# Second layer's first gates computed inside the attention projection's stage, and stage results stored through GpSimd's queue

## The chip, the core and the metric

The kernel runs on one core of a Trainium2 chip. A core has five engines, each with an instruction stream of its own, executed in order: TensorE (PE) multiplies matrices, VectorE (DVE) and ScalarE (ACT) work elementwise, GpSimd (POOL) does so more slowly, and SyncE (SP) issues most of the transfers between the chip's memory and the core's. GpSimd can issue transfers too, on a queue of its own. An instruction waits on semaphores for what it needs, and all behind it on its engine wait with it. The metric is the device time of one execution in microseconds, the median of several runs.

## The reference

One inference step of a two-layer trunk for two groups of requests: a prompt of 1024 positions, and 8 samples of 16 positions each, with width 1024 and everything in float32. Layer 0 mixes over time with an RWKV-7 recurrence. Layer 1 attends over a band: queries from its own projection, keys and values shared, computed once from the residual stream. Each layer ends in a gated feed-forward net. Cut to what the change touches:

```
def swiglu(h, w_gate, w_up, w_down):
    return (jax.nn.silu(h @ w_gate) * (h @ w_up)) @ w_down
...
for l in range(DEPTH):
    ...
    else:
        if l == N_A:
            k_new, v_new = shared_kv(x, c, ...)
        q = rms_norm((h @ p['wb_q'][j]).reshape(bsz, t, H_B, HEAD_B), p['q_norm'][j])
        o = band_attention(q, k_all, v_all, ...)
        out = o.reshape(bsz, t, d) @ p['wb_o'][j]
    x = x + gt_m[:, None, :] * out
    h = modulate(rms_norm(x, p['norm_ffn'][l]), sh_f, sc_f)
    x = x + gt_f[:, None, :] * swiglu(h, p['w_gate'][l], p['w_up'][l], p['w_down'][l])
```

## The kernel before

Activations lie feature-major: 128 features on the partitions, positions along the free dimension. The 1152 positions (1024 and 128 samples) are worked in two column halves, c=0 with 512 and c=1 with 640. A float32 product is made of three matmuls on rounded operands (`mm3`): `split` has ScalarE round a tile to `hi` (L330) and VectorE subtract it to get `lo` (L331).

The feed-forward net of a layer (`ffn`) runs over 22 groups f of hidden features. For each, `gate_up` makes seven products in place of eight by one step of Strassen's scheme. Their weights come from `strassen_weights(l, f)`: four loads of 256 KB (L1393), four additions (L1398 to L1401) and seven splits. Their other operands, B[c], come from `strassen_in`, once per half: eight loads of the normed residual X (L1351), the norm (`normed`: L411, and L419 to L421 for the samples), the combinations (L1357) and 28 splits. For the layer's f=0 the halves are computed apart, c=0 while c=1's operands are still being made; later groups do both at once. `gate_up` adds the products up (L1427), applies Silu and multiplies (L1441, L1443); its two results go to memory, s0 to the scratch tensor `bd`, s1 of f=0 to `b12` (`down_open`: `first`, `even` and `odd`, which make the second Strassen operands of each pair of groups). `down_sums` meanwhile prepares the weights of the down projection.

The stages in question follow one another: `kv` makes keys and values (to about 2400 us), `attention` runs the heads in pairs with the query projection and the first column half's output projection threaded between (to 2930), `attproj` does the second half's output projection in eight feature tiles n (to 2992), and then `ffn(1, ...)` begins. In `attproj`, `strassen_in` for c=0 advances by one step a tile (`next(sub, None)`), each tile's result is the residual plus the gated product (`residual`: L1228, L1232, L1233), is stored to `x3` (L2230), and its squares are added up for the next norm (`sq_add`, L369). After the last tile `sq_done` sums the squares over the partitions with a matmul against ones and takes the reciprocal root (`rsqrt2`, L391 and L392).

Results are stored from SP's queue: keys, values and queries (`head_tail`, `head_steps`, `out_v`, to the tensors out_kT, out_v and qT), attention outputs og (`heads_out`), the residual x3 (`proj_part`, `proj_rest`, `attproj`). Later loads read them back: the queries of the next pair of heads come as `h<-qT`, the attention outputs as `h<-og`.

The order of each engine's instructions is set at build time by a scheduler that simulates a timeline; the order in which the program is written gives the priority. On the chip each engine then takes its stream strictly in order. Tiles come from pools; a tile that takes the place of an older one waits for that one's last reader or writer.

## Time and profile before

| | us |
|---|---|
| median of 3 runs | 3776.3 |
| lowest and highest of them | 3771.32, 3779.6 |
| the profiled execution's own time | 3766.23 |
| its span, first to last instruction | 3764.4 |
| TensorE busy in the span | 3441.4 (91%) |
| VectorE, ScalarE, GpSimd busy | 2248.7, 1660.0, 787.5 |

The profile is of one execution. All durations below are of it, so a sum made from them stands against 3766.23, which is 10 us below the median of the runs. A line of a timeline gives the start, the duration, the engine, the line of the code (L12 is line 12), the operation, what is written and read, and in brackets the idle time before it with what ended it. SPq and POOLq mark the issue of transfers on SP's and GpSimd's queues. "Landing" is the time from the issue of a transfer to its completion.

### The profile page before, as it was taken

What the parts mean: (1) busy time and instruction counts of PE and PEld (TensorE: products, weight loads), DVE (VectorE), ACT (ScalarE), POOL (GpSimd) and SP (SyncE); (2) the same over time, 40 slices, a digit from 0 to 9 for tenths busy, and PEclk for the clock granted to TensorE, in tenths of its full rate; (3) what the DMA queues carried; (4) which work ended last, traced back from release to release, by engine and by line L of the source; (5) the groups of instructions that cost most, each with busy time, mean ns of one, the idle gap of its engine ahead of it and who ended that gap; (6) DMA issues with size and microseconds to landing.
All of it is one profiled execution on the core that took longest, in us unless ns stands there. A gap on an engine that the chain in (4) does not pass through costs nothing.

```text
span 3764.4 us, 74445 instructions
## 1 busy us (share of the span) xinstructions
PE 3441.4 (91%) x28982; PEld 3083.1 (82%) x28982; DVE 2248.7 (60%) x4366; ACT 1660.0 (44%) x3176; POOL 787.5 (21%) x775
## 2 busy tenths in 40 slices
PE   5888999999889799999999889789889899999999
PEld 4677778777667699999888869677667789999999
DVE  4667676765446765555446742666675675665655
ACT  5545556554223533333334542555564443333442
POOL 0000000000011066676100000000000146766200
PEclk9888899889699899999999999899999899999999
DMA  5776776677666444444889422445465434444764
GB/s 212 231 223 162 202 222 191 191 205 208 174 199 203 141 129 141 140 138 153 272 295 329 145 72 80 136 140 161 149 206 170 156 109 141 142 149 143 235 211 158
DMA packets 545938, 664.65 MB, mean 177 GB/s; under 512 B 137232, under 2 KB 405520, under 8 KB 541104
## 3 DMA queue, kind: packets, MB, share of 16 engines
q1 hardware_dynamic: 468736, 556.44, 46.5%
q0 software_dynamic: 23760, 85.08, 7.4%
q10 hardware_dynamic: 53088, 18.36, 2.1%
q8 instruction: 228, 3.74, 0.4%
q14 instruction: 126, 1.03, 0.1%
HBM read 483.18 MB, written 176.53 MB: 175 GB/s over the span
## 4 chain that ended last, share of the span: by engine, by line
PE 67%; DMA 13%; DVE 9%; issue 5%; ACT 4%; SPq 1%; POOL 1%; ACTq 0%; DVEq 0%; POOLq 0%
PE S L145 30%; PE PT L145 15%; PE acc L145 12%; PE st L145 3%; PE O L145 2%; PE G L145 1%; PE PT L2107 1%; PE aux L145 1%; DVE h L331 1%; PE Y L145 1%; DMA TT<-Z 1%; DMA raw<-in_wada 1%; DVE wlo L331 1%; DMA raw<-in_rw_o 1%; DMA aw<-in_wadb 1%
## 5 line engine op out<-in xcount | busy, mean ns | idle before, releaser
L145 PE MATMUL S<-h,w 128*128 128x256 f32 (+1 forms) x7374 | 1032.5, 299 | 24.8 <-ACT h L330 7.2
L145 PEld LDWEIGHTS S<-h,w 128*128 128x128 f32 x7374 | 1002.2, 191 | 43.2 <-issue 15.3
L330 ACT ACTIVATE w<-rq 128x512 fp32r<-128x512 f32 (+1 forms) x500 | 304.0, 614 | 645.8 <-PE S L145 259.6
L145 PE MATMUL acc<-mx,whi 128*128 128x384 f32 x1728 | 510.8, 373 | 31.6 <-ACT mx L330 12.3
L145 PE MATMUL PT<-h,w 128*128 128x256 f32 (+1 forms) x3714 | 527.4, 298 | 9.5 <-DVE h L331 3.5
L331 DVE TENSOR_TENSOR w<-rq,w 128x512 fp32r<-128x512 f32 (+1 forms) x500 | 384.7, 774 | 251.0 <-ACT w L330 212.6
L145 PEld LDWEIGHTS PT<-h,w 128*128 128x128 f32 x3714 | 505.3, 190 | 16.2 <-issue 6.5
L145 PEld LDWEIGHTS acc<-mx,whi 128*128 128x128 f32 x1728 | 339.7, 205 | 61.7 <-ACT mx L330 15.4
L145 PE MATMUL acc<-mx,wlo 128*128 128x384 f32 x864 | 318.0, 368 | 8.2 <-DVE wlo L331 8.2
L1427 POOL TENSOR_TENSOR t<-t,t 128x576 f32<-128x576 f32 (+1 forms) x132 | 221.9, 1683 | 263.0 <-ACT t L1434 153.3
L331 DVE TENSOR_TENSOR h<-h,h 128x1024 fp32r<-128x1024 f32 (+6 forms) x152 | 169.3, 1127 | 133.5 <-ACT h L330 120.6
L330 ACT ACTIVATE h<-h 128x1024 fp32r<-128x1024 f32 (+6 forms) x152 | 142.5, 950 | 158.8 <-DMA h<-bd 120.4
L145 PEld LDWEIGHTS acc<-mx,wlo 128*128 128x128 f32 x864 | 177.0, 205 | 19.7 <-DVE wlo L331 12.3
L331 DVE TENSOR_TENSOR wlo<-raw,whi 128x1024 fp32r<-128x1024 f32 x114 | 139.1, 1222 | 82.3 <-ACT whi L330 81.5
L330 ACT ACTIVATE whi<-raw 128x1024 fp32r<-128x1024 f32 x114 | 119.7, 1053 | 129.9 <-PE acc L145 73.0
L145 PE MATMUL S<-h,wh 128*128 128x320 f32 (+1 forms) x744 | 146.7, 351 | 19.5 <-ACT xo L1794 10.0
L145 PEld LDWEIGHTS S<-h,wh 128*128 128x128 f32 x744 | 123.6, 196 | 39.3 <-ACT xo L1794 15.8
L1427 DVE TENSOR_TENSOR t<-S,t 128x576 f32<-128x576 f32 (+1 forms) x117 | 86.7, 741 | 113.7 <-PE S L145 113.7
L145 PE MATMUL acc<-h,wh 128*128 128x256 f32 (+1 forms) x864 | 133.8, 303 | 3.5 <-DVE ht L391 1.3
L145 PEld LDWEIGHTS acc<-h,wh 128*128 128x128 f32 x864 | 118.0, 194 | 11.5 <-DVE ht L391 3.4
L1357 POOL TENSOR_TENSOR h<-h,h 128x256 f32<-128x256 f32 x12 | 10.7, 918 | 540.3 <-PE PT L145 540.3
L2108 ACT ACTIVATE pts<-PT 128x640 f32<-128x640 f32 (+4 forms) x128 | 72.6, 567 | 88.0 <-PE PT L2107 73.7
(480 smaller groups left out, 5536.4 us busy)
## 6 DMA issues: line engine op xcount, KB each, us to landing
bd<-t SPq DMA_DIRECT2D x154, 160.0 KB, 1.9
rq<-in_wg SPq DMA_DIRECT2D x88, 256.0 KB, 3.0
rq<-in_wu SPq DMA_DIRECT2D x88, 256.0 KB, 2.6
ws<-in_wd SPq DMA_DIRECT2D x64, 352.0 KB, 3.5
ws<-ws SPq DMA_DIRECT2D x64, 352.0 KB, 3.1
bd<-t SPq DMA_DIRECT2D x152, 128.0 KB, 1.8
rq<-ws SPq DMA_DIRECT2D x72, 256.0 KB, 3.2
h<-bd SPq DMA_DIRECT2D x28, 640.0 KB, 6.8
```

What stands on the lines that cost most here:

```text
L145: return nc.tensor.matmul(out, lhsT, rhs, start=start, stop=stop)
L330: self.nc.scalar.activation(hi, x, AF.Copy)
L331: self.nc.vector.tensor_tensor(lo, x, hi, ALU.subtract)
L1357: gp.tensor_tensor(out[j], x[j], y[j], op)
L1427: return eng.tensor_tensor(out, x, y, ALU.add)
L2107: nc.tensor.transpose(pt[:, j * 128:(j + 1) * 128], P[:, j * 128:(j + 1) * 128], self.C("ident"))
L2108: nc.scalar.activation(pts[:, 0:nk * 128], pt[:, 0:nk * 128], AF.Copy)
```

## The change

Two things are done.

First, f=0 of the second layer's gates, for c=0 only, is computed at the end of `attproj`. `early_weights` loads and splits its weights when the seventh feature tile (n=6) is written, into tiles that the attention no longer needs; c=0's operands are finished at the same point. After the reciprocal root, `gate_up` runs for c=0 with temporaries that lie in attention's buffers, its Silu behind the root's last ScalarE instruction. Its two stores go on GpSimd's queue. `ffn` for this layer then begins with f=2 (c=0, then c=1 after its operands), loads f=0's weights again for the missing c=1, and goes on with f=1, 3, 4 and so on to 21: 20 full groups in place of 21, over which the preparation of the down weights is spread. The first two pairs (f=0 with 1, f=2 with 3) reload the held half from memory; `b12` has two tensors.

Second, the stores named above (`head_tail`, `head_steps`, `out_v`, `proj_part`, `proj_rest`, `heads_out`, `attproj`) are issued by GpSimd in place of SP.

```diff
--- before.py
+++ after.py
@@ -387,7 +387,7 @@
         nc.scalar.activation(r, r, AF.Exp, scale=-0.5)
-        nc.scalar.activation(u, r, AF.Square, scale=float(n) ** -0.5)
+        self.rsq = nc.scalar.activation(u, r, AF.Square, scale=float(n) ** -0.5)
@@ -1303,6 +1303,7 @@
         self.halfraw = lambda: self.wq.tile([128, 512], F32, tag="rq", name=self.nm("rq"), bufs=5)
+        self.wtile = lambda: self.wq.tile([128, 512], F32R, tag="w", name=self.nm("w"), bufs=self.hw[2])
@@ -1383,7 +1384,7 @@
         def put(t):
-            hi, lo = (self.wq.tile([128, 512], F32R, tag="w", name=self.nm("w"), bufs=self.hw[2]) for _ in range(2))
+            hi, lo = (self.wtile() for _ in range(2))
@@ -1405,7 +1406,7 @@
 
-    def gate_up(self, put, B, W, cs):
+    def gate_up(self, put, B, W, cs, behind=None):
@@ -1429,7 +1430,8 @@
         add(dve, s0, product(1), t1)
-        nc.scalar.activation(s0, s0, AF.Silu)
+        with self.tc.issue_after(behind) if behind else ExitStack():
+            nc.scalar.activation(s0, s0, AF.Silu)
@@ -1446,14 +1448,18 @@
         nc = self.nc
-        spill = self.down_open(l)
-        self.gate_up(spill(0), B, iter(W), (0,))
+        spill = self.spill1 if l else self.down_open(l)
+        first = 2 if l else 0
+        self.gate_up(spill(first), B, iter(W), (0,))
...
             pass
-        self.gate_up(spill(0), B, iter(W), (1,))
-        for f in range(1, 22):
-            self.gate_up(spill(f), B, self.strassen_weights(l, f, nc.vector if f == 1 else None), (0, 1))
-            for g in range(32 * (f - 1) // 21, 32 * f // 21):
+        self.gate_up(spill(first), B, iter(W), (1,))
+        if l:
+            self.gate_up(spill(0), B, self.strassen_weights(l, 0, nc.vector), (1,))
+        for n, f in enumerate([1, *range(3, 22)] if l else range(1, 22)):
+            self.gate_up(spill(f), B, self.strassen_weights(l, f, nc.vector if l + n == 0 else None), (0, 1))
+            m = 20 if l else 21
+            for g in range(32 * n // m, 32 * (n + 1) // m):
@@ -1466,17 +1472,20 @@
         self.Ws = [self.dp.tile([128, 4, 1408], F32, name=f"ws{l}_{m}") for m in range(4)]
-        b12 = self.dp.tile([128, 576], F32, name=f"b12_{l}")
+        b12 = {p: self.dp.tile([128, 576], F32, name=f"b12_{l}_{p}") for p in range(l + 1)}
...
 
-        def first(s0, s1, cs):
-            c, = cs
-            nc.sync.dma_start(self.Bd[c][0][0][:, 0], s0)
-            nc.sync.dma_start(b12[:, part[c]], s1)
+        def first(p):
+            def f(s0, s1, cs):
+                c, = cs
+                q = nc.gpsimd if l and p + c == 0 else nc.sync
+                q.dma_start(self.Bd[c][0][0][:, p], s0)
+                q.dma_start(b12[p][:, part[c]], s1)
+            return f
@@ -1486,11 +1495,11 @@
             def f(s0, s1, cs):
-                if p == 0:
+                if p in b12:
...
                     for c in range(2):
-                        nc.sync.dma_start(held[0][:, part[c]], self.Bd[c][0][0][:, 0])
-                    nc.sync.dma_start(held[1], b12)
+                        nc.sync.dma_start(held[0][:, part[c]], self.Bd[c][0][0][:, p])
+                    nc.sync.dma_start(held[1], b12[p])
@@ -1504,7 +1513,7 @@
             return f
-        return lambda f: first if f == 0 else (odd if f % 2 else even)(f // 2)
+        return lambda f: (odd if f % 2 else first if f // 2 in b12 else even)(f // 2)
@@ -1775,12 +1784,11 @@
             with ExitStack() as c2:
-                A, st = self.attproj(B, x2, x3, self.attention(c2))
+                A, r = self.attproj(B, x2, x3, self.attention(c2))
...
                 self.wide_open2(c2, "1")
-                W = list(self.strassen_weights(1, 0, nc.vector))
-                r = self.sq_done(st)
+                W = list(self.strassen_weights(1, 2, nc.vector))
@@ -1824,7 +1832,7 @@
         yield from self.head_norm_steps(pz, m, g, x, self.one())
-        self.nc.sync.dma_start(dst, x)
+        self.nc.gpsimd.dma_start(dst, x)
@@ -1836,7 +1844,7 @@
         self.head_norm(pz, m, g, t, "acc")
-        self.nc.sync.dma_start(dst[:, n, 512 * c + o:512 * c + o + m], t)
+        self.nc.gpsimd.dma_start(dst[:, n, 512 * c + o:512 * c + o + m], t)
@@ -1891,7 +1899,7 @@
                     nc.scalar.activation(vt, pz, AF.Copy)
-                    nc.sync.dma_start(self.o["v"][4 * c + w, :, n * 256:(n + 1) * 256], vt)
+                    nc.gpsimd.dma_start(self.o["v"][4 * c + w, :, n * 256:(n + 1) * 256], vt)
@@ -1982,7 +1990,7 @@
                 self.residual(256, n, 64, t, x, pz)
-                self.nc.sync.dma_start(self.x3[:, n, o:o + 256], t)
+                self.nc.gpsimd.dma_start(self.x3[:, n, o:o + 256], t)
@@ -2006,7 +2014,7 @@
             self.residual(512, n, 64, x, x, pz)
-            nc.sync.dma_start(self.x3[:, n, 0:512], x)
+            nc.gpsimd.dma_start(self.x3[:, n, 0:512], x)
@@ -2127,7 +2135,7 @@
             nc.vector.tensor_copy(o[:, 0:w], O)
-            nc.sync.dma_start(self.og[n, :, t0:t0 + w], o[:, 0:w])
+            nc.gpsimd.dma_start(self.og[n, :, t0:t0 + w], o[:, 0:w])
@@ -2227,15 +2235,36 @@
             self.residual(512, n, 64, o, x, d)
-            nc.sync.dma_start(x3[:, n, self.cols(1)], o)
+            nc.gpsimd.dma_start(x3[:, n, self.cols(1)], o)
...
             next(sub, None)
-        for _ in sub:
-            pass
-        return A, st
+            if n == 6:
+                for _ in sub:
+                    pass
+                W0 = self.early_weights()
+        r = self.sq_done(st, self.rs[:, 0:640])
+        ends = iter([self.at.tile([128, 320], F32, tag=t, name=self.nm("t"), bufs=b) for t, b in [("ht", 5)] * 5 + [("xin", 2)]])
+        self.halfraw = lambda: next(ends)
+        self.spill1 = self.down_open(1)
+        self.gate_up(self.spill1(0), B, iter(W0), (0,), self.rsq.ins)
+        return A, r
+
+    def early_weights(self):
+
+        wide = [self.slot(1)[:, :1024] for _ in range(3)]
+        raws = iter([t[:, o:o + 512] for t in wide for o in (0, 512)])
+        pieces = [self.att("kc", [128, 4, 512], 1, F32R).rearrange("p a b -> p (a b)"),
+                  self.att("vc", [128, 4, 4, 128], 1, F32R).rearrange("p a b c -> p (a b c)"),
+                  self.slot(1, F32R)[:, :1024], self.slot(1, F32R)[:, :1024],
+                  *(self.att("bt", [128, 641], 3, F32R)[:, :512] for _ in range(2))]
+        tiles = iter([t[:, o:o + 512] for t in pieces for o in range(0, t.shape[-1], 512)])
+        self.halfraw, self.wtile, old = lambda: next(raws), lambda: next(tiles), self.halfraw
+        W = list(self.strassen_weights(1, 0, self.nc.vector))
+        self.halfraw = old
+        return W
```

Lines after the change are numbered by its own code: L1394 to L1402 stand for L1393 to L1401, L1428 for L1427, L1443 and L1445 for L1441 and L1443, L1352 for L1351, L1358 for L1357, and from attention on they are 8 higher.

The order of the instructions at three places. VectorE behind the residual of the projection's last tile, before the change; o is the tile's result, kk and rms the squares and the root, w and rq the weights' low parts and raw halves, x the loads X, h in the first row the sum of squares:

```order
L1233 TENSOR_TENSOR o_32737<-o_32737,x_32736 128x128
L369 TENSOR_TENSOR h_31922<-h_31922,kk_32743 128x640
L331 TENSOR_TENSOR w_32762<-rq_32753,w_32761 128x512
L331 TENSOR_TENSOR w_32766<-rq_32755,w_32765 128x512
L1398 TENSOR_TENSOR rq_32769<-rq_32757,rq_32759 128x512
L1399 TENSOR_TENSOR rq_32757<-rq_32753,rq_32757 128x512
L391 SCALAR_TENSOR_TENSOR kk_32798<-S_32794,kk_32798 128x640
L1400 TENSOR_TENSOR rq_32753<-rq_32769,rq_32753 128x512
L392 SCALAR_TENSOR_TENSOR rms_32797<-kk_32798,rms_32797 128x640
L1401 TENSOR_TENSOR rq_32755<-rq_32755,rq_32753 128x512
L419 TENSOR_TENSOR x_32804<-x_32804,rms_32797 128x128
```

The split of the next weights follows the sum of squares directly there. VectorE at the same place with the change; t are the early gate's temporaries, and the root lies in h_31922:

```order
L1233 TENSOR_TENSOR o_32768<-o_32768,x_32767 128x128
L369 TENSOR_TENSOR h_31922<-h_31922,kk_32774 128x640
L1428 TENSOR_TENSOR t_32787<-PT_32854,t_32786 128x256
L391 SCALAR_TENSOR_TENSOR kk_32780<-S_32777,kk_32780 128x640
L392 SCALAR_TENSOR_TENSOR h_31922<-kk_32780,h_31922 128x640
L1428 TENSOR_TENSOR t_32790<-PT_32897,t_32786 128x256
L1428 TENSOR_TENSOR t_32791<-S_32914,t_32790 128x256
L1443 TENSOR_TENSOR t_32788<-t_32788,t_32789 128x256
L1428 TENSOR_TENSOR t_32791<-S_32930,t_32791 128x256
L1445 TENSOR_TENSOR t_32787<-t_32787,t_32791 128x256
L331 TENSOR_TENSOR w_32963<-rq_32954,w_32962 128x512
L331 TENSOR_TENSOR w_32967<-rq_32956,w_32966 128x512
```

All additions of f=0's first half now stand ahead of the first weight split, which in both pieces is the first row with L331.

SP at the loads of X for c=1, before, with the semaphores that each row waits for (DMAHW are transfers of SP's queue, DMASW of GpSimd's; the others are engines):

```order
L1514 DMA ws_33723<-in_wd 128x4x176 [waits DMAHW6_49]
L1351 DMA x_32804<-x_110 128x640 [waits DMAHW7_49]
L1351 DMA x_32805<-x_110 128x640 [waits DMAHW0_49]
L1351 DMA x_32806<-x_110 128x640 [waits DMAHW1_49]
L1351 DMA x_32807<-x_110 128x640 [waits DMAHW2_49]
```

They wait for earlier transfers of SP's queue alone. SP at the same place with the change:

```order
L1394 DMA rq_32960<-in_wu 128x512
L1352 DMA x_32995<-x_110 128x640 [waits DMAHW4_49,PE_49]
L1352 DMA x_32996<-x_110 128x640 [waits DMAHW5_49,DMASW0_49,DVE_49]
L1352 DMA x_32997<-x_110 128x640 [waits DMAHW6_49,Activation_49]
L1352 DMA x_32998<-x_110 128x640 [waits DMAHW7_49,DMASW1_49,DVE_49]
```

The second and the fourth load now wait for transfers of GpSimd's queue and for VectorE: they use the buffers of the early gate's s1 and s0, whose stores are on that queue.

SP at one boundary between pairs of heads, before; bt, kc, vc, vn are biases and cached keys and values, og<-o, qT<-xin the stores of attention outputs and queries:

```order
L2040 DMA bt_29719<-in_rel 128x641
L2130 DMA og<-o_28887 128x128
L2130 DMA og<-o_28950 128x256
L1839 DMA qT<-xin_28953 128x320
L1927 DMA h_29028<-qT 64x1024
L1920 DMA h_29665<-out_kT 64x1024 x2
L2155 DMA kc_29412<-in_ck 128x2048
L2140 DMA qsm_29778<-qT 128x128
```

Three stores stand ahead of the load of the queries. SP at the same place with the change:

```order
L2165 DMA vn_29111<-out_v 16x4x128
L2048 DMA bt_29719<-in_rel 128x641
L1935 DMA h_29028<-qT 64x1024
L1928 DMA h_29665<-out_kT 64x1024 x2
L1935 DMA h_29670<-qT 64x1024
L2163 DMA kc_29412<-in_ck 128x2048
L2148 DMA qsm_29778<-qT 128x128
```

The three stores are gone from SP; the load of the queries, h<-qT, still stands ahead of the loads of the next pair, and that of the second half of the pair now also stands ahead of kc. GpSimd's stream, where the stores of that place now are:

```order
L1847 DMA qT<-xin_28784 128x320
L2138 DMA og<-o_28887 128x128
L1847 DMA qT<-xin_28953 128x320
L2138 DMA og<-o_28950 128x256
L1847 DMA qT<-xin_29188 128x256
```

They stand there in one row with no other work between them.

## The prediction

> **What bounds the kernel now.** The page comes first: its head, the busy times, and the chain that ended last.
>
> ```profile
> span 3764.4 us, 74445 instructions
> ...
> PE 3441.4 (91%) x28982; PEld 3083.1 (82%) x28982; DVE 2248.7 (60%) x4366; ACT 1660.0 (44%) x3176; POOL 787.5 (21%) x775
> ...
> PE 67%; DMA 13%; DVE 9%; issue 5%; ACT 4%; SPq 1%; POOL 1%; ACTq 0%; DVEq 0%; POOLq 0%
> ```
>
> TensorE is busy for 91% of the span and holds 67% of the chain, so an edit pays only where TensorE waits now. The table of stretches, cut at the stages that the change touches, shows where (microseconds, busy time and instructions of each engine, granted clock, DMA share, GB/s):
>
> ```profile
> 2500.00:2600.00 100.00, 91.08 (x795) 73.16 (x793) 64.48 (x192) 61.21 (x142) 0.00 (x0) 0.93 0.48 147
> ...
> 2985.00:3000.00 15.00, 11.68 (x66) 9.91 (x66) 5.52 (x10) 4.54 (x7) 0.00 (x0) 0.89 0.41 139
> 3000.00:3010.00 10.00, 3.92 (x23) 3.49 (x23) 9.48 (x21) 5.54 (x12) 0.00 (x0) 0.78 0.81 298
> 3010.00:3020.00 10.00, 7.43 (x51) 7.02 (x50) 10.00 (x28) 8.24 (x17) 1.11 (x1) 0.88 0.00 0
> 3020.00:3030.00 10.00, 5.92 (x37) 5.43 (x37) 10.00 (x26) 5.84 (x14) 2.61 (x2) 1.00 0.34 109
> 3030.00:3043.00 13.00, 10.99 (x49) 9.84 (x50) 12.61 (x30) 5.47 (x14) 2.11 (x2) 0.74 0.06 19
> ...
> 3100.00:3500.00 400.00, 400.00 (x3009) 400.00 (x3008) 235.88 (x271) 131.26 (x217) 273.87 (x230) 1.00 0.46 145
> ```
>
> Between the projection and the second layer's gates, from 3000 to 3043, VectorE is the full engine (9.48 of 10, then 10.00, 10.00 and 12.61 of 13) and TensorE the one that waits. In the gates' steady loop it is the reverse: 400.00 of 400 on TensorE. There 3009 matmuls take 400 us, 0.133 us each. One feature group f of the gates has 168 matmuls (7 products, 4 slices, 3 matmuls, two halves c), so a full f costs 22.3 us, and, divided by columns (256 to 320), c=0 9.9 us and c=1 12.4 us. TensorE's timeline around the transition:
>
> ```profile
> 2987.74 4.27 PE L145 MATMUL PT<-h,wh 128*128 128x320 f32 x28
> 2995.16 2.24 PE L145 MATMUL S<-h,cst 128*128 128x320 f32 x4 [3.15 <-DVE h L369]
> 2997.58 2.41 PE L145 MATMUL S<-h,w 128*128 128x256 f32 x12 [0.18 <-ACT w L330]
> ...
> 3042.75 6.66 PE L145 MATMUL S<-h,w 128*128 128x256 f32 x48
> ```
>
> Call the end of the projection's matmuls T = 2987.74 + 4.27 = 2992.0. From T, TensorE needs 2.24 us for the sum of squares and 22.3 us for f=0, and f=1 starts at 3042.75 = T+50.7. So 26 us are lost here, and this is what the early gates aim at. VectorE's timeline gives the cause:
>
> ```profile
> 3000.48 0.69 DVE L1398 TENSOR_TENSOR rq<-rq,rq 128x512 f32<-128x512 f32 x1 [1.00 <-DMA rq<-in_wu]
> ...
> 3041.33 0.48 DVE L331 TENSOR_TENSOR h<-x,h 128x320 fp32r<-128x320 f32 x1
> ```
>
> From 3000.48 (T+8.5) to the last split of c=1's operands at 3041.8 VectorE runs 41.3 us without a gap.
>
> **The change part by part.** *Projection.* Group f=0's weights are now loaded and split during the last feature tiles: 7 splits and 4 additions on VectorE, 7 copies on ScalarE, 4 loads of 256 KB on SP's queue. What VectorE does there now, by form, in 2950 to 2992:
>
> ```profile
> L331 DVE TENSOR_TENSOR h<-h,h 128x256 fp32r<-128x256 f32 x14 | 8.3, 642 | 0.4 <-ACT h L330 0.4
> L331 DVE TENSOR_TENSOR wh<-vf,wh 128x512 fp32r<-128x512 f32 x9 | 6.5, 726 | 8.9 <-ACT wh L330 8.9
> ```
>
> Added is 7 x 0.73 + 4 x 0.69 = 7.9 us to some 25 us of 42 (these rows and the smaller ones), so it fits beside TensorE, which is the busier one. A split that lands ahead of a tile's own can hold it up by one or two: I take +0.5 us on T; bounds 0 and +3 (four such hold-ups).
>
> *After T.* Counting VectorE's rows in the changed order: the tile's residual, the sum of squares, then everything that ends f=0's first half, and only then the first weight split of f=2. So TensorE first does the ones product (T+3.2 to T+5.4, as now) and six of c=0's seven products, 6 x 1.42 us, to T+13.9, or T+14.4 with the clock of 0.89 that the row of 2985 to 3000 shows for part of it. Two additions on GpSimd and two on VectorE follow, and VectorE turns to f=2 at T+16.3, where it started on f=0 at T+8.5 before. Its block until the last operand split is of the same kinds: two more weight splits, three fewer additions, and the two rows of the reciprocal root gone; 39.5 us in place of 41.3. To that comes a new wait. The loads of X, eight in a row,
>
> ```profile
> 2997.01 5.91 SPq L1351 DMA_DIRECT2D x<-x  x8
> ```
>
> need buffers that the early gate's temporaries held: the second waits for the store of the gate's s1 on GpSimd's queue, the fourth for that of s0, and the other six stand behind them on SP. The store is issued at T+15.8. What a store costs on each queue I read from these rows (2100 to 3050; size, median us from issue to landing):
>
> ```profile
> x<-x SPq DMA_DIRECT2D x16, 320.0 KB, 4.3
> ...
> x<-xin SPq DMA_DIRECT2D x16, 128.0 KB, 3.3
> ...
> qT<-xin SPq DMA_DIRECT2D x12, 160.0 KB, 1.8
> ...
> x<-h POOLq DMA_DIRECT2D x6, 128.0 KB, 2.7
> ```
>
> 2.7 us to land and 4.3 us for the load behind it: the second X is there at T+22.8, while VectorE has run out of other work at T+20.5. It idles 2.3 us. The block then ends at T+16.3+39.5+2.3 = T+58.1; f=2's last product ends 1 us later, as now (3041.8 against 3042.75), and f=0's second half needs 12.4 us: T+71.5 with two groups done. Before, two groups are done at T+50.7+22.3 = T+73.0. **The gates' part gains 1.5 us**, not the 9.9 us of the products moved: VectorE, which binds, begins 7.8 us later. Bounds: a gain of 4 (no wait for X), a loss of 3 (7.1 us for the store in place of 2.7, the longest landing below).
>
> *Steady loop.* f=0's weights are loaded and split a second time (1 MB, 5 us of VectorE), f=3 reloads its held pair, and the sums for the down weights spread over 20 rounds. TensorE covers all: VectorE is at 235.88 of 400 there and the DMA engines at 0.46. Zero. If cover failed, it would be in the 12.4 us of a lone c=1 half, where 7 splits and some 2 us of additions still fit:
>
> ```profile
> L331 DVE TENSOR_TENSOR w<-rq,w 128x512 fp32r<-128x512 f32 x126 | 106.6, 846 | 63.1 <-ACT w L330 44.0 <-PE S L145 12.7 <-PE PT L145 6.4
> ```
>
> *The stores.* In the kv projection and attention they leave SP for GpSimd, which is idle (0.00 in the row of 2500 to 2600). Each costs it 542 ns of issue:
>
> ```profile
> L1588 POOL DMA_DIRECT2D x<-h x32: 542/542/587, 1869.5 to 2134.4; - x32
> ...
> DMA to landing us min/median/max: 2.4/3.6/7.1
> ```
>
> It counts where a load reads what a store has just written. The chain of waits in attention has such places:
>
> ```profile
> 2405.47 1.76 DMA qT<-xo
> 2407.93 4.20 DMA h<-qT
> ...
> 2601.63 1.76 DMA qT<-xin
> 2603.45 3.49 DMA h<-qT
> ...
> 2779.07 1.80 DMA qT<-xin
> 2780.95 3.39 DMA h<-qT
> ...
> 2850.04 3.75 DMA h<-og
> ...
> 2911.07 3.21 DMA x<-xin
> 2914.30 4.23 DMA h<-x
> ```
>
> About seven in all (five pair boundaries with qT, one with og, one with x). The store lands in 1.76 to 1.80 us on SP; on GpSimd's queue, 2.7 by the nearest row, so +0.9 each and 6 us if each stood bare. SP is relieved in turn: it no longer stops for results, and loads that stand behind a store go out when their own buffer is free. But the loads of qT stay ahead of the bias, cache and value loads in its order, and they wait for the landing. About half of the places had slack or gain from a free SP: I take **+2 us**; bounds +12.6 (3.6 against 1.8, seven times) and -8 (below).
>
> [...]
>
> **Sum.** +0.5 - 1.5 + 0 + 2 = +1.0 us, on the profiled execution's own 3766.2: 3767.2. That execution was 10 us (0.27%) below the median of 3776.3, a spread of runs and not of the work, so the term goes on the median: **3777**.
>
> **The rivals.** *Free SP* (faster). If the stores were what held the loads up, the four long waits of TensorE that DMA ends at pair boundaries shrink. For: on SP, og's stores land anywhere from 1.7 to 9.6 us,
>
> ```profile
> DMA to landing us min/median/max: 1.7/2.6/9.6
> ```
>
> TensorE's idle times there, in the brackets:
>
> ```profile
> 2413.31 0.69 PE L145 MATMUL S<-h,h 128*128 128x128 f32 x2 [7.18 <-DVE h L331]
> ...
> 2535.31 1.43 PE L145 MATMUL acc<-ht,cst 128*128 128x320 f32 x2 [2.31 <-ACT ht L1797]
> ...
> 2666.94 0.33 PE L2107 MATMUL PT<-cst,P 128*128 128x128 f32 x1 [3.30 <-ACT pts L2108]
> ...
> 2724.14 1.33 PE L2107 MATMUL PT<-cst,P 128*128 128x128 f32 x5 [3.69 <-ACT pts L2108]
> ```
>
> Half of these 16.5 us is -8; with the gates at -1.5 and the projection at +0.5, -9: 3767. Against: qT's loads still wait in SP's order for the very stores that moved.
>
> *Late stores* (slower). The seven places pay the other row's median, 3.6 against 1.8, +12.6, and X comes 0.9 us later: -1.5 + 0.9 + 0.5 + 12.6 = +12.5, 3789. It decides as soon as a store on GpSimd's queue lands 1.4 us later than on SP at all seven places (+10 and more). For: the row of 2.4/3.6/7.1. Against: the six of 2.7 nearest in time, and 3.3 us for SP's own stores of x.
>
> *No gain from the gates.* If X waits longer (7.1 us for the store, loss of 3), the sum is +5.5, 3782: still no change that can be told.
>
> **How the numbers follow.** A measurement of this kernel can tell about 0.2%, 7.5 us, from no change. Free SP 0.22; late stores 0.27; the rest, forecast and lost gates, 0.51. Faster 0.23, same 0.50, slower 0.27. The range takes in both rivals with 3 us beyond each: 3764 to 3792.
>
> **What would show it.** Right: VectorE's first weight split of f=2 about 16 us after the projection's last matmul, a wait of it for X of 2 to 3 us, and two groups done 70 to 73 us after T; qT's stores landing in 2.5 to 3 us. Wrong: if the two groups are done before T+68, the block of VectorE was shorter than counted; if TensorE's idle time from 2400 to 2930 falls by 5 us or more, SP's waits were the bound; if it grows by 8, the landing was. The steady loop must stay at a full TensorE.

## The result, and the profile after

The change makes the kernel **slower by 0.51%**: 3795.69 us, the median of 8 runs (3784.47 to 3807.43), against 3776.8 us, the median of 8 runs of the kernel before. The ratio is 1.0051 with a 95% interval of 1.0033 to 1.0068, so 12 to 26 us. The forecast of 3777 is wrong, and 3795.69 lies above its range.

The page of the changed kernel, its head, TensorE's busy time and the chain that ended last (the execution's own time is 3805.07 us):

```profile
span 3803.3 us, 74561 instructions
...
PE 3455.2 (91%) x28982; PEld 3090.9 (81%) x28982; DVE 2263.4 (60%) x4383; ACT 1665.9 (44%) x3188; POOL 884.7 (23%) x937
...
PE 57%; issue 18%; DMA 10%; DVE 9%; ACT 3%; POOL 2%; SPq 1%; ACTq 0%; POOLq 0%; DVEq 0%
```

The same 28982 matmuls take 13.8 us more, and the span grows by 38.9. The two busy shares look alike; where the time went is read from rows at the same place of the program in both. TensorE's timeline, first before, then after: attention's first matmul of a query head, its last one of a pair, and (after alone; before's are in the prediction) the projection's last matmuls and the first ones behind two finished groups of gates.

```profile
2405.01 1.12 PE L145 MATMUL O<-h,cst 128*128 128x512 f32 x2 [1.31 <-ACT h L1797]
...
2881.90 1.08 PE L145 MATMUL PT<-vc,pts 128*32 128x128 f32 x32 [0.85 <-ACT pts L2108]
```

```profile
2421.30 1.12 PE L145 MATMUL O<-h,cst 128*128 128x512 f32 x2 [1.31 <-ACT h L1805]
...
2915.02 1.08 PE L145 MATMUL PT<-vc,pts 128*32 128x128 f32 x32 [0.85 <-ACT pts L2116]
...
3021.34 7.20 PE L145 MATMUL PT<-h,wh 128*128 128x320 f32 x48
...
3098.64 3.36 PE L145 MATMUL PT<-h,w 128*128 128x256 f32 x24
...
3136.74 4.99 PE L145 MATMUL S<-h,w 128*128 128x256 f32 x24 [1.95 <-DVE t L1428]
```

| stretch | before, us | after, us | difference |
|---|---|---|---|
| up to attention's first row | 2405.0 | 2421.3 | +16.3 |
| attention, first row to last | 476.9 | 493.7 | +16.8 |
| to the projection's last matmul, T (2992.0 and 3028.5) | 110.1 | 113.5 | +3.4 |
| T to two groups of gates done | 73.0 | 70.1 | -2.9 |
| from there to the end | 699.3 | 704.7 | +5.4 |

The first stretch is almost all unchanged code, and this execution is 9 us above its own median. A kernel below whose code is before's up to there (before with late pins) has 2417.9 us in it, so most of those 16 us are the spread of executions. Attention is where the change shows, though the spread of executions is in its 16.8 us too. Cut at TensorE's rows `PT<-vn,pts`, about 4.4 us of it lie in attention's first piece, ahead of every place that is looked at below, 3.6 in the second, 2.3 at the boundary where ScalarE stands longest, 4.4 at the last boundary and 3.6 in the two pieces that end the stage; the other pieces together give some 1.5 back. Take the last boundary first. Between two marks there (the rows `PT<-vn,pts` that begin at 2769.26 and 2792.43 before, 2794.25 and 2821.82 after), the table of stretches has, before and then after (us, busy time and instructions of PE, PEld, DVE, ACT, POOL, granted clock, DMA share, GB/s):

```profile
2769.20:2792.40 23.20, 18.18 (x189) 12.80 (x181) 14.95 (x52) 14.48 (x36) 0.00 (x0) 1.00 0.78 265
```

```profile
2794.20:2821.90 27.70, 22.21 (x191) 16.06 (x189) 14.88 (x50) 15.70 (x36) 2.17 (x4) 0.82 0.80 274
```

From row to row the same piece costs 4.4 us more, and TensorE's busy time in the two stretches differs by 4.0: TensorE stands once, and comes back at a lower clock. Both are 14.1 us behind the first mark when it begins to wait; the wait is 2.6 us longer after, and the rows behind it take 1.8 us more. The same columns in slices, after:

```profile
2806.00:2809.00 3.00, 2.38 (x21) 1.36 (x21) 1.71 (x7) 0.70 (x1) 0.00 (x0) 1.00 0.63 147
2809.00:2812.00 3.00, 0.52 (x3) 0.30 (x5) 1.13 (x1) 2.22 (x4) 0.00 (x0) 0.73 0.90 343
2812.00:2815.00 3.00, 3.00 (x22) 2.67 (x22) 1.20 (x5) 0.84 (x5) 0.00 (x0) 0.50 1.05 399
2815.00:2818.00 3.00, 3.00 (x14) 1.94 (x13) 1.64 (x6) 1.68 (x4) 0.54 (x1) 0.50 1.05 386
```

ScalarE's timeline of the piece says why TensorE stands, before and then after:

```profile
2780.90 0.70 ACT L2108 ACTIVATE pts<-PT 128x640 f32<-128x640 f32 x1 [0.64 <-PE O L145]
...
2783.15 0.70 ACT L2108 ACTIVATE pts<-PT 128x640 f32<-128x640 f32 x1 [1.54 <-PE PT L2107]
...
2784.36 1.06 ACT L330 ACTIVATE h<-h 64x1024 fp32r<-64x1024 f32 x1 [0.51 <-DMA h<-qT]
```

```profile
2806.08 0.70 ACT L2116 ACTIVATE pts<-PT 128x640 f32<-128x640 f32 x1 [1.86 <-PE O L145]
2809.78 1.06 ACT L330 ACTIVATE h<-h 64x1024 fp32r<-64x1024 f32 x1 [3.00 <-DMA h<-qT]
2810.74 0.68 ACT L2116 ACTIVATE pts<-PT 128x640 f32<-128x640 f32 x1
```

The row `ACT L330 h<-h 64x1024` of each is the point. It is `split`'s rounding of the next pair's queries, just loaded back from `qT`. Before, it stands behind both `pts` copies (the transposed softmax of the present pair); after, **one of them stands behind it**. The load has not landed and ScalarE takes its stream in order, so it stands 3.00 us, the ready `pts` with it, and TensorE, which needs that copy:

```profile
2811.48 0.48 PE L2115 MATMUL PT<-cst,P 128*128 128x128 f32 x1 [3.10 <-ACT pts L2116]
```

At the same row before TensorE had waited 0.49. At another boundary ScalarE stands longer (ScalarE, TensorE, and the issue of the store and of the load behind it, after; TensorE's wait there was 3.30 us before, a row that the prediction shows):

```profile
2685.99 1.06 ACT L330 ACTIVATE h<-h 64x1024 fp32r<-64x1024 f32 x1 [7.89 <-DMA h<-qT]
2686.95 0.68 ACT L2116 ACTIVATE pts<-PT 128x640 f32<-128x640 f32 x1
```

```profile
2687.69 1.33 PE L2115 MATMUL PT<-cst,P 128*128 128x128 f32 x5 [5.00 <-ACT pts L2116]
```

```profile
2680.13 0.54 POOL L1847 DMA_DIRECT2D qT<-xin  x1 [3.77 <-DVE xin L1811]
```

```profile
2682.40 0.46 SPq L1935 DMA_DIRECT2D h<-qT  x1
```

The load is issued 2.27 us behind the store, and ScalarE goes on 3.6 us after that. Nothing is unusual in the transfers: before, this store was issued at 2656.84 and its load at 2658.96, 2.12 us, and the store landed in 2.1 us on either queue. ScalarE was sent to wait sooner: it began to wait at 2678.10, 2.0 us ahead of the store's issue, where before it had come 4.5 us behind it (at 2661.34, for 1.29 us). Over the attention, ScalarE's wait for these loads (total us, times, longest), before and after:

```profile
ACT h L330 <- DMA h<-qT: 15.1, 8, 6.0
```

```profile
ACT h L330 <- DMA h<-qT: 24.1, 8, 7.9
```

And the landing itself, on GpSimd's queue (KB each, median us):

```profile
og<-o POOLq DMA_DIRECT2D x28, 128.0 KB, 2.2
...
qT<-xin POOLq DMA_DIRECT2D x12, 160.0 KB, 2.1
...
qT<-xin POOLq DMA_DIRECT2D x12, 128.0 KB, 2.2
```

Before, the same three were 2.3, 1.8 and 1.7 on SP.

### The profile page after: what moved, and what is told of

Read it like the earlier page. It is cut to its first block, busy times and chain, and to the rows that moved or that the text cites. A ratio compares the mean times of both kernels' runs of the same rounds, so it can differ in the third digit from the quotient of the medians.

```text
span 3803.3 us, 74561 instructions
## 1 busy us (share of the span) xinstructions
PE 3455.2 (91%) x28982; PEld 3090.9 (81%) x28982; DVE 2263.4 (60%) x4383; ACT 1665.9 (44%) x3188; POOL 884.7 (23%) x937
## 4 chain that ended last, share of the span: by engine, by line
PE 57%; issue 18%; DMA 10%; DVE 9%; ACT 3%; POOL 2%; SPq 1%; ACTq 0%; POOLq 0%; DVEq 0%
PE S L145 27%; PE PT L145 13%; PE acc L145 9%; PE st L145 3%; PE G L145 1%; DVE h L331 1%; PE aux L145 1%; DMA TT<-Z 1%; PE O L145 1%; DVE w L331 1%; PE Y L145 1%; DVE wlo L331 1%; DMA raw<-in_rw_o 1%; DMA Z<-T 1%; DMA h<-bd 1%
## 5 line engine op out<-in xcount | busy, mean ns | idle before, releaser
L145 PE MATMUL S<-h,w 128*128 128x320 f32 (+1 forms) x7314 | 1027.8, 299 | 31.4 <-ACT h L330 7.9
L330 ACT ACTIVATE w<-rq 128x512 fp32r<-128x512 f32 (+1 forms) x500 | 304.0, 615 | 623.4 <-PE S L145 263.9
L331 DVE TENSOR_TENSOR w<-rq,w 128x512 fp32r<-128x512 f32 (+1 forms) x500 | 393.7, 793 | 249.6 <-ACT w L330 219.6
L1428 POOL TENSOR_TENSOR t<-t,t 128x576 f32<-128x576 f32 (+2 forms) x135 | 225.6, 1672 | 267.7 <-ACT t L1436 169.6
L331 DVE TENSOR_TENSOR h<-h,h 128x1024 fp32r<-128x1024 f32 (+7 forms) x154 | 170.7, 1123 | 143.2 <-ACT h L330 136.5
L330 ACT ACTIVATE h<-h 128x1024 fp32r<-128x1024 f32 (+6 forms) x154 | 143.7, 947 | 175.6 <-DMA h<-bd 125.7
L331 DVE TENSOR_TENSOR wlo<-raw,whi 128x1024 fp32r<-128x1024 f32 x114 | 139.3, 1223 | 88.8 <-ACT whi L330 87.8
L330 ACT ACTIVATE whi<-raw 128x1024 fp32r<-128x1024 f32 x114 | 119.8, 1055 | 139.4 <-PE acc L145 70.5
L145 PEld LDWEIGHTS S<-h,wh 128*128 128x128 f32 x744 | 124.4, 197 | 41.7 <-ACT xo L1802 15.8
L1428 DVE TENSOR_TENSOR t<-S,t 128x576 f32<-128x576 f32 (+2 forms) x119 | 87.0, 731 | 108.8 <-PE S L145 108.7
L2115 PE MATMUL PT<-cst,P 128*128 128x128 f32 x480 | 81.2, 292 | 37.4 <-ACT pts L2116 27.2
```

The lines of the kernel that those rows point to most:

```text
L145: return nc.tensor.matmul(out, lhsT, rhs, start=start, stop=stop)
L330: self.nc.scalar.activation(hi, x, AF.Copy)
L331: self.nc.vector.tensor_tensor(lo, x, hi, ALU.subtract)
L1428: return eng.tensor_tensor(out, x, y, ALU.add)
L2115: nc.tensor.transpose(pt[:, j * 128:(j + 1) * 128], P[:, j * 128:(j + 1) * 128], self.C("ident"))
```

## The experiments

Two theories stood at the start. **Landing**: the stores land later on GpSimd's queue, and the loads behind them too. **Order**: with the stores off SP the build's scheduler computes other ready times, and puts the queries' splits ahead of softmax steps that could run; on the chip their load is not there yet. In all runs below the whole computation is done. `issue_after(i)` puts an instruction behind i in the same engine's stream and adds no wait.

**Which half of the change.** One kernel has only the seven kinds of stores on GpSimd, one only the early gates.

```diff
 # stores only, in the kernel before; likewise at the other six places
-        self.nc.sync.dma_start(dst, x)
+        self.nc.gpsimd.dma_start(dst, x)
 # gates only, in the change; likewise at the other six places
-        self.nc.gpsimd.dma_start(dst, x)
+        self.nc.sync.dma_start(dst, x)
```

> The kernel before with the seven kinds of result stores on GpSimd's queue and no early gates. Theory (the stores cost, nearly all of it in attention): attention and the projection (2400 to 2992 us of the profile before) last about 20 us longer, the rest is unchanged, 3797 us. Rival (the early gates cost, and attention's longer time is chance of one execution): 3777 us and attention within 4 us of before.

> The changed kernel with the seven kinds of stores back on SP's queue; the early gates and their own two stores on GpSimd stay. Theory (the stores cost): attention as before, the stretch from the projection's last matmul to the end of two groups 1 to 4 us shorter, 3 to 5 us lost later in the gates' loop, 3779 us. Rival (the early gates cost): 3796 us.

Stores alone 1.0032 [1.0018, 1.0047], gates alone 0.9997 [0.9983, 1.0011]. The loss is the stores'; the gates neither gain nor lose. In the first, ScalarE's wait for `h<-qT` is 22.7 us, near the change's 24.1. Attention takes 486.7 us in its one profiled execution, 9.8 more than before; 20 for attention and the projection had been expected.

**Which stores.** The change with part of them back on SP: first those of keys and queries (`head_tail`, `head_steps`), then og and x3 instead.

```diff
 # head_tail and head_steps
-        self.nc.gpsimd.dma_start(dst, x)
+        self.nc.sync.dma_start(dst, x)
 # the other kernel: heads_out, proj_part and proj_rest
-            nc.gpsimd.dma_start(self.og[n, :, t0:t0 + w], o[:, 0:w])
+            nc.sync.dma_start(self.og[n, :, t0:t0 + w], o[:, 0:w])
```

> The changed kernel with the stores of queries and keys alone (head_tail, head_steps) back on SP's queue. Theory (the cost sits where a pair of heads waits for its queries): of the 17 us that attention lost some 13 come back, 3783 us. Rival (each moved store costs its share, 24 of 75 moved stores of attention): 5 us come back, 3791 us.

> The changed kernel with the stores of attention outputs and of the first column half's residual (heads_out, proj_part, proj_rest) back on SP's queue; those of queries stay on GpSimd's. Theory (the queries): only the places where og and x3 are read back gain, 3 to 6 us, 3791 us. Rival (each moved store its share, 51 of 75): 12 us come back, 3784 us.

With the heads' stores on SP 1.0008 [0.9995, 1.0021], with og and x3 on SP 1.0039 [1.0023, 1.0055]. The loss is in the heads' stores. They are the ones that the splits' loads wait for, so both theories still stand.

**Landing or order.** The next two kernels are to tell them apart. One kernel keeps all stores on GpSimd (the first one above) and holds the queries' splits behind the softmax step that they followed before; its counterpart keeps the stores on SP, as before, and holds softmax steps behind the split.

```diff
-        self.split(t[0:64], t[64:128], raw)
+        with self.tc.issue_after(self.marks[at].ins):
+            self.qsplit(*self.late.pop(at))
 # the counterpart: the softmax step behind the split's instruction
-        nc.scalar.activation(pts[:, 0:nk * 128], pt[:, 0:nk * 128], AF.Copy)
+        with self.held(("T", n, 2 * qt + e)):
+            x = nc.scalar.activation(pts[:, 0:nk * 128], pt[:, 0:nk * 128], AF.Copy)
```

> The kernel with the stores alone on GpSimd's queue (no early gates), and the splits of the queries (the copy on ScalarE of what h<-qT has loaded) pinned behind the softmax step that they followed in the kernel before, for pairs 1, 3, 4, 5 and 7. Theory (order: the scheduler placed these splits 1 to 4 softmax steps earlier, where the load has not landed yet, and ScalarE's later steps wait behind them): attention's loss of 9 us falls to 4 or less, about 3786 us on a chip where the kernel before takes 3782. Rival (landing: a store on GpSimd's queue lands later): attention keeps its loss, 3793 us.

> The kernel before, all stores on SP's queue, with the softmax steps that followed the split of the queries in the changed kernel held behind it (pairs 1, 3, 4 and 7, as far as the order allows): the changed order with the old queue. Theory (order): attention loses 4 to 9 us, 3786 to 3791 us. Rival (landing): nothing is lost, 3782 us.

All stores on GpSimd with nearly before's order (the splits stand as before, or 1 to 4 softmax rows behind): 1.0008 [0.9993, 1.0022], from 1.0032. Stores on SP with the splits one row ahead at four of the seven boundaries, and nothing else: 1.0025 [1.0005, 1.0044]. So the order alone costs time on SP's queue, though the interval only just leaves out 1, and most of the loss of the stores alone goes with the order. The profiled executions do not bear the first out: attention takes 487.0 us in it, as long as with the stores alone (486.7), which is the sign that the landing theory had asked for; with the changed order on SP it takes 490.7, against 476.9 before. A single execution is good to about 10 us here (last section), so the timed ratios decide, and they leave the two theories less cleanly parted than hoped. ScalarE's wait in the first (the split is L1938 there):

```profile
ACT h L1938 <- DMA h<-qT: 14.1, 8, 6.6
```

That is before's 15.1, with a store that lands in 2.1 to 2.6 us.

**The gates and the pins in the whole change.** Three kernels follow. The first is the gates alone with two suspected waits taken out (the early weights loaded after the last tile, X's buffers free of the gate's stores). The second is the whole change with its splits pinned, that is held behind a softmax step, as in the kernel above. The third is the first with the early weights' splits behind the reciprocal root.

```diff
 # the first: after the loop over the tiles, and two temporaries elsewhere
-                W0 = self.early_weights()
+        W0 = self.early_weights()
...
+        ends = iter([ends[0], self.spare[:, 512:768], self.spare[:, 768:1024], *ends[1:]])
 # the third, besides
+        with self.tc.issue_after(self.rsq.ins):
+            W0 = self.early_weights()
```

> The early gates with the stores on SP's queue, the early weights issued after the last feature tile has been written in place of after the seventh, and the gate's s0 and s1 in a buffer that the loads of X do not use. Theory (the early weights' splits ahead of the tiles' own held the projection up by 3 us, and X waited 2 us for the store): 3 to 5 us faster than the early gates alone, 3775 us where the kernel before takes 3782. Rival (VectorE's block sets the end of the transition and the projection's delay was chance): no different from the early gates alone, 3779 us.

> The changed kernel with the splits of the queries pinned as in the run of the stores alone. Theory (order): attention's 17 us fall by 6 to 10, 3788 us where the kernel before takes 3782. Rival (landing): unchanged, 3797 us.

> The refined early gates (stores on SP's queue), with ScalarE's part of the early weights queued behind the last ScalarE step of the first reciprocal root of the projection. Theory (the early weights' splits stand inside the root's chain and wait there for their load): the projection's 4 us come back, in the trace the root's second step follows its first at once; 3776 us where the kernel before takes 3780. Rival (the projection is held up by what the early weights load and split later): no different from the refined gates, 3782 us.

Their ratios are 1.0002 [0.9986, 1.0018], 1.0032 [1.0016, 1.0048] and 1.0009 [0.9992, 1.0025]. None gains on before, and the second returns less than its theory asked. The weights' split does stand in the root's chain (ScalarE, gates alone):

```profile
2934.00 0.69 ACT L388 ACTIVATE rms<-S,eps 128x512 f32<-128x512 f32 x1 [2.31 <-PE S L145]
2936.38 0.63 ACT L330 ACTIVATE kc<-h 128x512 fp32r<-128x512 f32 x1 [1.68 <-DMA h<-in_wg]
2936.91 0.61 ACT L389 ACTIVATE rms<-rms 128x512 f32<-128x512 f32 x1
```

It makes 2.91 us from the first to the third row out of before's 0.72, but taking it out returned no time that can be told, and in the whole change's profile it does not stand there: 0.73 us. The second of the three kernels is a miss that was not resolved: pair by pair the queries stand there as before or 1 to 4 softmax rows behind, and 0.3% remains.

**Later than before.** If a split that waits for its load is the trouble, it can be put where the load has surely landed: keys' and queries' splits of the next pair behind the second and fourth `pts` of the pair before. This is done in the whole change (with the root's pin), in the gates with the root's pin, and in the kernel before.

```diff
-        self.split(t[1], t[2], raw)
+        self.pinned(("T", n - 1, 1), e, t[1], t[2], raw)
...
-        self.split(t[0:64], t[64:128], raw)
+        self.pinned(("T", n - 1, 3), e, t[0:64], t[64:128], raw)
```

> The changed kernel, all stores on GpSimd's queue, with the early weights queued behind the root and the splits of the next pair's keys and queries pinned into the pair before (behind its softmax steps 1 and 3), where the load has landed long since. Theory (order): what the stores cost goes, 3776 to 3782 us where the kernel before takes 3780. Rival (landing, or the queue itself): 3790 us or more remain.

> The refined gates behind the root, stores on SP's queue, and the late pins of the run above. Theory (order, also in the kernel before: ScalarE waits there for keys and queries while softmax steps stand behind): faster than both kernels, 3770 us where the kernel before takes 3780. Rival (those waits are covered): as without the pins, 3776 us.

> The kernel before with the late pins alone. Theory (order): TensorE's waits behind the splits at the boundaries go, 4 to 8 us faster, 3774 us where the kernel before takes 3780. Rival (covered): 3780 us.

The change with them: 0.9990 [0.9972, 1.0009]. **The whole loss is gone, with every store still on GpSimd's queue.** The other two, 0.9999 [0.9982, 1.0016] and 0.9996 [0.9980, 1.0011], gain nothing, a miss for the hope of beating before: there ScalarE's waits fell as far (to 6.5 us in the second), but the times did not follow. That the change with late pins loses nothing does not part the two theories, since a split that stands this late would not wait for a late landing either; it shows that the loss comes through the places where these splits wait. In the change, the query split has no idle time ahead of it any more, and the waits view has 8.3 us (ScalarE's timeline, then the view):

```profile
2687.85 0.38 ACT L2128 ACTIVATE pts<-PT 128x256 f32<-128x256 f32 x1 [0.64 <-PE PT L2127]
2688.13 1.04 ACT L330 ACTIVATE h<-h 64x1024 fp32r<-64x1024 f32 x1
```

```profile
ACT h L330 <- DMA h<-qT: 8.3, 3, 6.6
```

**Which of the three pins.** That kernel held three things. So each was held alone in the change, and the queries' also in the kernel with only the heads' stores on GpSimd, which had lost 0.39% while its ScalarE waited only 15.8 us.

> The change with only the splits of the next pair's first queries held behind the fourth softmax step of the pair before (pts, steps counted from 0: step 3); keys' splits and the early weights stay where the scheduler puts them. Order theory, queries alone: the loss of the changed kernel (1.005) is theirs, so within 0.15% of before (0.9985 to 1.0015), and ScalarE's wait for h<-qT falls from 24 us to under 12. Rival, keys' splits or the early weights carry it: 1.003 or more.

> The change with only the splits of the next pair's first keys held behind the second softmax step of the pair before; queries' splits where the scheduler puts them. Order theory, queries alone: 1.003 to 1.006, ScalarE's wait for h<-qT still above 16 us. Rival, the keys' splits carry the loss: within 0.15% of before.

> The change with only the early weights' splits held behind the reciprocal root at the end of the attention; attention's order as in the change. Order theory: 1.003 to 1.006, since the root's chain is worth 2 to 3 us at most. Rival, the early weights' splits carry the loss: within 0.15% of before.

> The kernel with keys', values' and queries' stores on GpSimd (og and x3 back on SP; 1.0039 without the pin) with the queries' splits held as in the first of these. Order theory, queries alone: within 0.15% of before. Rival, what that kernel lost came from the stores' landing or from the queue they share: 1.003 or more.

Queries alone 1.0007 [0.9993, 1.0020], keys alone 1.0017 [1.0003, 1.0031], root alone 1.0039 [1.0023, 1.0054], queries with the heads' stores 1.0007 [0.9995, 1.0020]. The queries' splits carry the loss in both kernels. The keys' pin returned part of it against what was expected, and the trace shows how: with the keys held, the scheduler put the queries back at before's place or up to 2 rows behind it at six of the seven boundaries. The number of ScalarE's softmax rows (`P` and `pts`) that stand ahead of the split of each next pair's first queries, counted in the traces:

| kernel | stores of heads | rows ahead, seven boundaries | wait for h<-qT, us | ratio |
|---|---|---|---|---|
| before | SP | 14, 38, 76, 115, 153, 187, 230 | 15.1 | 1 |
| the change | GpSimd | 12, 39, 75, 113, 149, 191, 229 | 24.1 | 1.0051 |
| stores only | GpSimd | 12, 39, 75, 113, 149, 191, 229 | 22.7 | 1.0032 |
| root's pin alone | GpSimd | 12, 39, 75, 113, 149, 191, 229 | 23.5 | 1.0039 |
| og and x3 on SP | GpSimd | 12, 39, 75, 115, 153, 191, 231 | 15.8 | 1.0039 |
| heads on SP | SP | 14, 38, 76, 115, 153, 187, 229 | 18.0 | 1.0008 |
| changed order on SP | SP | 13, 38, 75, 114, 153, 187, 229 | 17.8 | 1.0025 |
| keys' pin alone | GpSimd | 14, 39, 77, 115, 153, 189, 229 | 16.3 | 1.0017 |
| stores only, old order | GpSimd | 14, 39, 77, 115, 153, 191, 230 | 14.1 | 1.0008 |
| the change, old order | GpSimd | 14, 39, 77, 115, 153, 191, 230 | 13.5 | 1.0032 |
| queries' pin alone | GpSimd | 13, 51, 89, 127, 165, 203, 241 | 7.8 | 1.0007 |
| all three pins | GpSimd | 13, 51, 89, 127, 165, 203, 241 | 8.3 | 0.9990 |

Kernels with splits ahead of before's place at two boundaries or more lose 0.25 to 0.5%, on either queue; those with splits far behind it (from the second boundary on) lose at most 0.07%, on GpSimd's queue. At or near before's place it is 0.08 to 0.17%, with one that does not fit, the change with the old order (0.32%). In the means, with the heads' stores on GpSimd, splits ahead lose 0.40% (four kernels) and splits near before's place 0.19% (three). With these stores on SP, splits ahead lose 0.25% (one kernel), and splits at or one row from before's place 0.04% (heads on SP and the three gates kernels without late pins). So by these means the order is worth about 0.2% on either queue, though each single ratio is uncertain by some 0.15%. Some 0.15% between the queues is left at like places; no run says whether that is the landing, and it goes too when the splits stand late. The wait's total alone does not rank the kernels: 15.8 us went with a loss of 0.39%, and before's 15.1 were covered.

The seventh boundary, the one shown first above, can be read in all 18 profiles by the same two marks of TensorE. In the six kernels with the split one row ahead (229) the piece takes 25.4 to 28.2 us, on either queue, but for 23.2 with the heads' stores on SP; in the seven with 230 or 231 it takes 23.2 to 25.5; in the five with late splits 21.1 to 24.2.

## Why the prediction was wrong, step by step

*What bounds the kernel*: right. The transition lost 26 us to VectorE and the steady loop was TensorE's. After the change 150 us of it read

```profile
3150.00:3300.00 150.00, 150.00 (x1129) 150.00 (x1129) 92.76 (x103) 48.98 (x81) 108.34 (x89) 1.00 0.47 152
```

*Projection, +0.5 with bounds 0 to +3*: mis-sized. The profiled execution has +3.4, just outside; the gates alone has 113.6 in the same stretch, but the stores alone, without early gates, has 113.4 too, so the early weights are not shown to be its cause. In the change's profile 2.7 of the 3.4 us are TensorE's waits for the splits of the projection's own weights (`wh`) behind the first root, 8.4 us in place of 5.7. That is the kind of hold-up that the prediction named. The split in the root's chain above, which it did not see, is in the gates alone only.

*Gates, -1.5 with bounds -4 to +3*: right. VectorE's first weight split of f=2 and its wait for X:

```profile
3043.35 1.29 DVE L331 TENSOR_TENSOR w<-rq,w 128x512 fp32r<-128x512 f32 x2
...
3048.02 0.29 DVE L419 TENSOR_TENSOR x<-x,h 128x128 f32<-128x128 f32 x1 [0.39 <-DMA x<-x]
```

The split comes at T+14.8 (forecast T+16.3), two groups are done at T+70.1 (forecast T+71.5, before T+73.0). X was waited for 0.39 us and not 2.3, so VectorE's own block was the longer term. The early products that left TensorE's path are paid for in its idle time behind them, as the prediction said: VectorE, not TensorE, sets this stretch (from 3043.4 to 3083 VectorE is busy 39.17 of 39.60 us, TensorE 26.23). With the projection's loss the two cancel in these rows; 0.9997 for the gates alone agrees, with an interval of 5 us either way.

*Steady loop, 0*: nearly. 5.4 us later from there to the end, of which 1.95 is the wait in TensorE's last row at the top (3136.74); a single execution, not followed further.

*Stores, +2 with bounds -8 to +12.6*: **this is the step that failed.** The term of +2 measured +12 us by itself (1.0032, the stores alone), and the whole change +19 where the sum said +1. The prediction priced the landing (0.9 us, seven places) and let half of it hide in slack. The landing rose by only 0.3 for qT's 160 KB and 0.5 for its 128 KB, and fell by 0.1 for og: less than priced. What the prediction did not price is that **the stores' queue is an input of the scheduler**, and that moving them re-orders ScalarE: at five of the seven boundaries the split of the queries then stood 1 to 4 softmax rows further ahead, and ScalarE's wait for them went from 15.1 to 24.1 us. It looked at the new order of VectorE at the transition and of SP and GpSimd at a boundary, and took ScalarE's order in the attention as given, though the stores there were the only edit. How much of the 19 us is this order, and how much the landing, is not settled (below). With VectorE busy 60% of the span the stores of qT landed in 2.1 to 2.2 us (medians), where the nearest rows of before had suggested 2.7 to 3.6. The longest took 7.1 us, against 6.5 on SP before.

*The rivals*: late stores came nearest in size (3789). Its own condition, 1.4 us later at all seven places, was not met, at the longest stand the store took 2.1 us on both queues, and the kernel with all stores on GpSimd and nearly the old order has no loss that can be told; but the change with that order keeps 0.32%, so a share of it is not excluded. Free SP fell: TensorE's idle time grew from 70.7 to 81.9 us over the attention's some 3870 matmuls (span less PE in these sums of the table of stretches, before from 2400 to 2924 and after from 2416.3 to 2957).

```profile
sum 524.00, PE 453.29 PEld 363.03 DVE 327.26 ACT 295.40 POOL 0.20; mean PE 226.65 PEld 181.51 DVE 163.63 ACT 147.70 POOL 0.10
```

```profile
sum 540.70, PE 458.84 PEld 367.48 DVE 328.28 ACT 295.69 POOL 47.34; mean PE 229.42 PEld 183.74 DVE 164.14 ACT 147.84 POOL 23.67
```

One of the four waits that it built on was not of its kind: ahead of TensorE's 2.31 us at 2535.31 ScalarE had stood 2.09 us for weights (`h<-in_wq`). The sign of "if it grows by 8, the landing was" would have misled: it grew, and a landing later by 0.3 to 0.5 us does not make up for it.

*What stays open*: stores alone lose 0.32%, gates alone nothing, both together 0.51%. The intervals allow for that, and no run settles whether the rest is a loss of its own. Why the change with the old order still lost 0.32% is open too, and with it the share of the queue at an unchanged order. That the loss comes through the queries' splits is shown, on GpSimd's queue and with one pin (1.0007). That their new place is the reason is shown for the order on SP, and otherwise by the trace at single boundaries.

## What to carry to other kernels

Where a scheduler sets the order at build time, moving a transfer to another queue is an edit to every engine's stream: compare the order of the in-order engines in the stage that the transfer feeds, and look for an instruction that waits for a load and now stands ahead of ready work. An instruction that consumes a stored and reloaded tile can be pinned behind work that is ready; here that alone took 1.0051 to 1.0007. And if two stages each look unchanged in cost, price the place of the waiting instruction, not the length of its wait.

## What was not expected of the hardware

A short stand can cost TensorE more than its length, by the granted clock. In the slices of the last boundary's piece, after, the clock is 1.00 up to the stand of 3.10 us and 0.50 for the 6 us behind it, where the rows take 1.8 us more. Not every wait does this: before, in the same piece, a wait of 1.53 us left the clock at 1.00. Nor is the clock always back after the same time. At attention's start the same ten matmuls stand in before's timeline and then in after's as

```profile
2433.00 1.45 PE L145 MATMUL acc<-h,wh 128*128 128x256 f32 x10
```

```profile
2452.47 2.50 PE L145 MATMUL acc<-h,wh 128*128 128x256 f32 x10
```

They take 1.72 times as long after; the granted clock there is 1.00 before and 0.50 after. In both it had been lower for a while: the table of stretches has 0.50 from 2411 to 2432 before and from 2427 to 2455 after, and 1.00 from 2433 and 2456 on. TensorE's stands of 7.18 us before and 7.78 us after end at 2413.31 and 2430.21, so the clock is back some 19 us behind the one and 25 us behind the other. The last waits ahead of the ten matmuls are one of 1.82 us in both and two more of 0.23 and 0.24 in after alone; whether the two short ones made the difference no run shows.

Single executions spread more than the place of the query splits tells: the gates with the root's pin and the gates alone have the same place for every query split in the attention, and it took 487.4 and 476.8 us in them. No run shows why. The length of a stage in one profile is thus good to about 10 us in this kernel, which is why the experiments are judged by their timed ratios and the profile by its order and its waits.
